# Gate rows of a hybrid decoder block stored in DRAM as 2-KB runs, in four copies side by side

## The chip, the cores and the metric

The kernel runs on one core of one Trainium2 chip. Time is the device time of one execution in microseconds (us). The engines are TensorE (PE; its weight loads are listed apart as PEld), VectorE (DVE), ScalarE (ACT), GpSimd (POOL) and SyncE (SP); SP and POOL issue the DMA transfers, which all run on the core's 16 DMA engines.

## The reference

One layer of a decoder block on 512 tokens with 1024 channels, all in float32. A combined projection of the normalised input gives the operands of two branches. Branch A is a gated delta rule over 8 heads, in chunks of 64 tokens; branch B is causal attention over 8 heads ("FOX") with a forget bias. Both need per-token, per-head gate values, and the change is about how these are spread:

```
u = RMSNorm(x)
[q_A,k_A,v_A,z_A,a_A,b_A | q_B,k_B,v_B,f_B | gate_A,gate_B] = u @ W_in
beta = sigmoid(b_A);  g = -exp(a_log) * softplus(a_A + dt_bias)      # per token and head
A: S_t = a_t (I - beta_t k_t k_t^T) S_{t-1} + beta_t k_t v_t^T,  o_t = S_t^T q_t,  a_t = exp(g_t)
B: softmax(q k^T / sqrt(d) + c_t - c_s),  c = cumsum(log sigmoid(f_B)),  causal
m = sigmoid(gate_A) * (y_A @ P_A) + sigmoid(gate_B) * (y_B @ P_B);  h = x + m @ W_out
out = h + relu(RMSNorm(h) @ W_up)^2 @ W_down
```

The decay between two tokens of a chunk is the exponential of a difference of cumulated g. As a 128x128 block with keys on the partitions and queries along the row, it needs one of the two as a column (a value per partition) and the other as a row that is the same on all partitions.

## The kernel before

Matrix products run on PE with each float32 operand split into a high and a low part (`hi`, `lo`: ACT casts `hi`, DVE subtracts for `lo`) and three products. Weights come as "units" of 128x1024 through three raw buffers. The program is one sequence of units. First come the gates' columns (`w_ab`) and five `z` units, then the projections q, k, v of heads 0 to 3 of branch A (`w_gdn`, lines 281 to 285), the other three `z` units, and a stream of three Strassen chunks with seven products each that makes q, k, v of FOX heads 0 to 3 (`w_sf`, line 986), with the first projections of heads 4 and up in between. A second such stream (`w_st`) makes FOX heads 4 to 7 and the output gates; the block's output projections and the MLP (`mlp`, line 1147) follow. In a chunk some weight quarters are loaded from SP, the others are formed by loads on POOL's queue that add to a raw buffer (`sraw<-w_sf`, line 225).

Beside the units run small tasks (generators) that give way to each other at each unit: `gates`, `decays` for each group of four heads, `head` for each head of branch A, the inversion and scan of a group, and `fox_worker`. The order of the instructions on each engine is then set by a scheduler at build time. Each engine works its instructions in that order.

`gates` turns the gate columns into four kinds of row per head, with 512 tokens each: exp of the cumulated decay (kind 0), beta (1), the centred cumulated decay (2) and minus the cumulated log forget gate (3). It holds them with tokens on the partitions, one column for each kind, chunk of 128 tokens and head. One transpose on PE gives kinds 0 to 2 as 96 rows of 128 tokens (`rowsT`, lines 523 to 525), another kind 3 as 32 rows (`rowsF`). They are stored to DRAM (`rowd`, laid out kind, chunk, head, token), the first from POOL's queue (line 526), the second from SP's (line 546). `row_page` loads one row onto all 128 partitions, from SP (line 550): each partition reads the same four pieces of 512 bytes, which stand 4 KB apart in `rowd`. There are 32 such loads, one for each kind and head.

Their users are: `decays`, where POOL masks kind 2 (`em`, line 585), ACT takes exp (line 589) and POOL multiplies by kind 1 (`eb`, line 591); `head`, where DVE forms `AT` from `eb` (line 644) and POOL multiplies q by kind 0 (`er`, line 655); and `fox_worker`, where POOL masks kind 3 (`nd`, line 884) and ACT adds it as bias. The row pages share four buffers. `head` also has its norm's power on POOL (`ssk`, line 351), between these. Finished operands of a head are stored to DRAM (`hd<-conv`, `hd<-kn`, `hd<-vb`, `hd<-am`, line 148) and come back for the scan; `zc` loads and `oad` stores belong to the scan's output.

Of the kernel before, what the change touches and what calls it, by code (L numbers as in the profile page):

```python
# [7 lines left out]
F32 = mybir.dt.float32  # L8
F32R = mybir.dt.float32r
AF = mybir.ActivationFunctionType  # L10
ALU = mybir.AluOpType
# [4 lines left out]
P = 128  # L16
T = 512
D = 1024
KT = D // P
H = 8  # L20
NCH = T // P
# [5 lines left out]
LA_RAW_MLP = 5  # L27
PER_UNIT = 2
PIN = (400, 400, 0)
NMM = 3  # L30
NZX = 5
DECAY_AT = (9, 1)
# [11 lines left out]
def hybrid_block(tc, a, out):  # L44
    nc = tc.nc
# [6 lines left out]
    drp = ctx.enter_context(tc.tile_pool(name="drp", bufs=1, space=DRAM))  # L52
    mix = ExitStack()
    cm = mix.enter_context(tc.tile_pool(name="cm", bufs=1))
    rwp = mix.enter_context(tc.tile_pool(name="rwp", bufs=4))
# [3 lines left out]
    swp = mix.enter_context(tc.tile_pool(name="swp", bufs=2))  # L59
    pmm = ctx.enter_context(tc.tile_pool(name="pmm", bufs=NMM, space=PSUM))  # L60
    psx = ExitStack()
    pat = psx.enter_context(tc.tile_pool(name="pat", bufs=8 - NMM, space=PSUM))

    n_names = [0]

    def nm(s):
        n_names[0] += 1
        return f"{s}_{n_names[0]}"
# [5 lines left out]
    def page(dt=F32, s="pg"):  # L74
        if s in FOX_TAGS:
            return fxp.tile([P, T], dt, tag=s, name=nm(s))
        tag = TAGS_OF.get(s, s)
        if tag in TAGS:
            return pgp.tile([P, T], dt, tag=tag, name=nm(s), bufs=TAGS[tag])
        return pgp.tile([P, T], dt, tag="pg", name=nm(s))  # L80
# [3 lines left out]
    def const(shape, s, dt=F32):  # L84
        return (cp if s in KEEP else cm).tile(shape, dt, tag=s, name=s)
# [3 lines left out]

    mmfree = [f"mm{i}" for i in range(NMM)]  # L90

# [9 lines left out]
    def atps(s="at"):  # L101
        return pat.tile([P, T], F32, tag="at", name=nm(s))

    def v3(ap, n):
        return ap.rearrange("p (a b) -> p a b", a=n)

    def bc(ap, n):
        return ap.unsqueeze(2).to_broadcast(list(ap.shape) + [n])

    def cs(c):  # L110
        return slice(c * P, (c + 1) * P)

    mm = nc.tensor.matmul
    vec, act, pool = nc.vector, nc.scalar, nc.gpsimd
# [23 lines left out]
    def start(gen):  # L138
        tasks.append(gen)
        return gen  # L140
# [166 lines left out]
    ident = const([P, P], "ident")  # L307
# [52 lines left out]
    def inv_rms(pss, rs, rb):  # L360


        for c in range(NCH):
            vec.tensor_scalar(rs[:, c:c + 1], pss[:, c * 64:c * 64 + 1], 1.0 / D, EPS, op0=ALU.mult, op1=ALU.add)
        rsq(rs, rs)
        yield
        prb = atps("rb")
        for c in range(NCH):
            mm(prb[:, cs(c)], rs[:, c:c + 1].to_broadcast([P, P]), ident, start=True, stop=True)
        act.copy(rb, prb)  # L370
# [21 lines left out]
    for pool_, tag, n in early:  # L392
        t = pool_.tile([P, n * T], F32R, tag=tag, name=nm("xs"))
# [63 lines left out]
    beta = const([P, NCH, H], "beta")  # L457
    gf = const([P, NCH, 16], "gf")
    ngc = const([P, NCH, H], "ngc")
    kds = const([P, NCH, H], "kds")  # L460
    dec = const([P, NCH, H], "dec")
    nbe = const([P, NCH, H], "nbe")
    cc = const([P, NCH, H], "cc")
    rowd = drp.tile([4, NCH, H, P], F32, tag="rowd", name="rowd")

    def rowc(t):
        return t[:, :].unsqueeze(1).to_broadcast([P, NCH, H])

    def gates(ps):
        abT = page(s="abT")  # L470
        act.copy(abT[:64, :], ps[:64, :])
        yield from inv_rms(pss, rs, rb)
        start(normalise())
        yield
        pt = atps("abt")
        for c in range(NCH):
            mm(pt[:, c * 32:(c + 1) * 32], abT[:64, cs(c)], blk_id[0:64, :], start=True, stop=True)
        ab = const([P, NCH, 32], "ab")
        vec.tensor_tensor(ab, v3(pt[:, 0:NCH * 32], NCH), bc(rs[:, :], 32), op=ALU.mult)
        act.activation(beta, ab[:, :, 8:16], AF.Exp, scale=-1.0)  # L480
        aexp = const([P, H], "aexp")
        act.activation(aexp, alog, AF.Exp)
        yy = const([P, NCH, 16], "yy")
        vec.tensor_tensor(yy[:, :, 0:8], ab[:, :, 0:8], rowc(dtb), op=ALU.add)
        vec.tensor_tensor(yy[:, :, 8:16], ab[:, :, 16:24], rowc(fbias), op=ALU.add)
        vec.tensor_scalar(yy[:, :, 8:16], yy[:, :, 8:16], -1.0, None, op0=ALU.mult)

        ee = const([P, NCH, 16], "ee")
        vec.scalar_tensor_tensor(ee, yy, -1.0, yy, op0=ALU.mult, op1=ALU.min)
        act.activation(ee, ee, AF.Exp)  # L490
        yield
        vec.tensor_scalar(beta, beta, 1.0, None, op0=ALU.add)
        vec.reciprocal(beta, beta)
        zz = const([P, NCH, 16], "zz")
        vec.tensor_scalar(zz, ee, 2.0, None, op0=ALU.add)
        vec.reciprocal(zz, zz)
        vec.tensor_tensor(zz, zz, ee, op=ALU.mult)
        vec.tensor_tensor(ee, zz, zz, op=ALU.mult)
        pp = const([P, NCH, 16], "pp")
        vec.tensor_scalar(pp, ee, 1.0 / 19, None, op0=ALU.mult)  # L500
        for k in (17, 15, 13, 11, 9, 7, 5, 3):
            vec.scalar_tensor_tensor(pp, pp, 1.0 / k, ee, op0=ALU.add, op1=ALU.mult)
        vec.scalar_tensor_tensor(pp, pp, 1.0, zz, op0=ALU.add, op1=ALU.mult)
        vec.tensor_scalar(yy, yy, 0.0, None, op0=ALU.max)
        vec.scalar_tensor_tensor(gf, pp, 2.0, yy, op0=ALU.mult, op1=ALU.add)
        vec.scalar_tensor_tensor(gf[:, :, 0:8], gf[:, :, 0:8], -1.0, rowc(aexp), op0=ALU.mult, op1=ALU.mult)
        vec.tensor_scalar(gf[:, :, 8:16], gf[:, :, 8:16], -1.0, None, op0=ALU.mult)
        yield
        pc = atps("cum")
        mm(pc[:, 0:64], upper, gf[:, :, :].rearrange("p a b -> p (a b)"), start=True, stop=True)  # L510
        mm(pc[:, 64:128], ones, gf[:, :, :].rearrange("p a b -> p (a b)"), start=True, stop=True)
        cum = const([P, NCH, 16], "cum")
        vec.tensor_copy(cum, v3(pc[:, 0:64], NCH))
        mm(pc[:, 128:160], mid, gf[:, :, 0:8], start=True, stop=True)
        tot = const([P, NCH, 16], "tot")
        vec.tensor_copy(tot, v3(pc[:, 64:128], NCH))

        rows = const([P, 4, NCH, H], "rows")
        vec.tensor_copy(rows[:, 2], v3(pc[:, 128:160], NCH))
        act.activation(rows[:, 0], cum[:, :, 0:8], AF.Exp)  # L520
        vec.tensor_copy(rows[:, 1], beta)
        pt = atps("rowsT")
        nc.tensor.transpose(pt[:96, 0:P], rows[:, 0:3, :, :].rearrange("p k c h -> p (k c h)"), ident)
        rowsT = const([96, P], "rowsT")
        vec.tensor_copy(rowsT, pt[:96, 0:P])
        nc.gpsimd.dma_start(rowd[0:3, :, :, :].rearrange("k c h t -> (k c h) t"), rowsT)
        vec.tensor_scalar(ngc, rows[:, 2], -1.0, None, op0=ALU.mult)
        yield
        early_rows[0] = True
        vec.tensor_copy(cc[:, 0], cum[:, 0, 8:16])  # L530
        pre = const([P, NCH, H], "pre")
        vec.tensor_copy(pre[:, 1], tot[:, 0, 8:16])
        for c in range(2, NCH):
            vec.tensor_tensor(pre[:, c], pre[:, c - 1], tot[:, c - 1, 8:16], op=ALU.add)
        vec.tensor_tensor(cc[:, 1:], cum[:, 1:, 8:16], pre[:, 1:], op=ALU.add)
        vec.tensor_scalar(rows[:, 3], cc, -1.0, None, op0=ALU.mult)
        vec.tensor_tensor(kds, tot[:, :, 0:8], cum[:, :, 0:8], op=ALU.subtract)
        act.activation(kds, kds, AF.Exp)
        act.activation(dec, tot[:, :, 0:8], AF.Exp)
        vec.scalar_tensor_tensor(nbe, beta, -1.0, rows[:, 0], op0=ALU.mult, op1=ALU.mult)  # L540
        yield
        pt = atps("rowsT")
        nc.tensor.transpose(pt[:32, 0:P], rows[:, 3, :, :].rearrange("p c h -> p (c h)"), ident)
        rowsF = const([32, P], "rowsF")
        vec.tensor_copy(rowsF, pt[:32, 0:P])
        nc.sync.dma_start(rowd[3, :, :, :].rearrange("c h t -> (c h) t"), rowsF)

    def row_tile(src, v=None):
        t = rwp.tile([P, T], F32, tag="row", name=nm("row"))
        nc.sync.dma_start(v3(t[:, :], NCH) if v else t, src)  # L550
        return t

    def row_page(kind, h):
        return row_tile(rowd[kind, :, h, :].partition_broadcast(P), True)


    G = 4
# [655 lines left out]

    pq = ctx.enter_context(tc.tile_pool(name="pq", bufs=8 - NMM, space=PSUM))
    free = [(pq, f"pq{i}") for i in range(8 - NMM)] + [(pmm, tag) for tag in mmfree]

# [149 lines left out]
    for k, (w, c, p, s_) in enumerate(MLP):  # L1366
        for pin, first in zip(pins, PIN):
            pin[0] = k >= first
# [4 lines left out]
        n = pos[0]  # L1373
# [119 lines left out]
```

## Time and profile before

| what | value |
|---|---|
| time, median of 3 runs (lowest to highest) | 982.0 us (980.56 to 983.99) |
| profiled execution: its time, its span | 986.59 us, 984.8 us |
| mean granted PE clock | 0.993 |
| row loads from `rowd` | 32, from 69.9 to 360.7 us |
| DMA, mean over the span | 180 GB/s |

The profile lists, for each engine, when an instruction ran, how long it took, and in brackets how long the engine stood idle before it and what ended that. A group row ends with total busy time and the mean ns of one. A window row has the busy times of PE, PEld, DVE, ACT and POOL with their instruction counts (or of one engine where it is said), then the granted PE clock, the share of the 16 DMA engines' time in use, and GB/s. A DMA's row on SPq or POOLq is its issue, not its transfer; the time to landing is from the issue until the data is there.

### The profile page before, as it was taken

To read this page: it belongs to the slowest core of one execution; us is meant where nothing else is said; L and a number is where in the kernel's file an instruction comes from. 1 tells how busy PE (TensorE), PEld (TensorE's weight loads), DVE (VectorE), ACT (ScalarE), POOL (GpSimd) and SP (SyncE) were. 2 spreads that over 40 slices of the span, in tenths; PEclk is the share of its full clock that TensorE was granted. 3 is DMA by queue.
4 is the path that set the end of the run, shared out by engine and by line. 5 is a ranking of instruction groups with operands and counts; after the bars stand their busy time and mean duration, and the time that the engine had idled before them with its cause. 6 is when DMAs were issued, how large, how long until landed. Compare 5 with 4: busy or idle time off the path is not lost.

```text
span 984.8 us, 17110 instructions
## 1 busy us (share of the span) xinstructions
PE 966.0 (98%) x6460; PEld 868.2 (88%) x6460; DVE 724.8 (74%) x1220; ACT 625.3 (63%) x1086; POOL 231.7 (24%) x232
## 2 busy tenths in 40 slices
PE   8999997999998999999999999999999999999998
PEld 6788787998897899999999888889989989988986
DVE  6877976875557889965656625889897697698596
ACT  6888754687656676777656422578855765666761
POOL 1504221240242423521230004412021121121110
PEclk9999998999999999999999999999999999999999
DMA  7346957763677787777878735678798788889884
GB/s 264 126 138 171 262 144 174 163 183 105 201 225 186 167 202 172 149 167 193 223 174 223 264 107 164 124 184 165 200 182 194 189 170 208 181 173 203 182 165 123
DMA packets 96625, 177.01 MB, mean 180 GB/s; under 512 B 8048, under 2 KB 53264, under 8 KB 96544
## 3 DMA queue, kind: packets, MB, share of 16 engines
q1 hardware_dynamic: 80352, 117.15, 37.9%
q0 software_dynamic: 16192, 58.78, 34.1%
q8 instruction: 51, 0.84, 0.3%
q14 instruction: 30, 0.25, 0.1%
HBM read 156.96 MB, written 18.94 MB: 179 GB/s over the span
## 4 chain that ended last, share of the span: by engine, by line
PE 86%; DMA 4%; DVE 4%; ACT 2%; issue 2%; POOL 1%; SPq 0%; DVEq 0%; POOLq 0%; ACTq 0%
PE mlp L1147 35%; PE st L986 19%; PE mm L281 6%; PE mm L285 6%; PE mm L282 6%; DMA row<-rowd 2%; PE fo L950 2%; PE sc L925 2%; DMA sraw<-w_sf 1%; PE pT L941 1%; PE v L801 1%; DVE conv L602 1%; DMA zc<-zd 1%; PE o L822 1%; DVE lo L263 1%
## 5 line engine op out<-in xcount | busy, mean ns | idle before, releaser
L1378 ACT CAST hi<-draw 128x1024 fp32r<-128x1024 f32 x124 | 130.0, 1050 | 118.5 <-PE mlp L1147 99.5
L1385 DVE TENSOR_TENSOR lo<-draw,hi 128x1024 fp32r<-128x1024 f32 x124 | 151.3, 1223 | 45.7 <-ACT hi L1378 42.5
L262 ACT CAST hi<-sraw 128x1024 fp32r<-128x1024 f32 x70 | 73.2, 1047 | 69.0 <-PE st L986 34.0
L1147 PE MATMUL mlp<-hi,shi 128*128 128x512 f32 x280 | 109.5, 391 | 0.1
L1147 PE MATMUL mlp<-hi,slo 128*128 128x512 f32 x280 | 109.1, 390 | 0.0
L1147 PE MATMUL mlp<-lo,shi 128*128 128x512 f32 x280 | 109.1, 390 | 0.0
L263 DVE TENSOR_TENSOR lo<-sraw,hi 128x1024 fp32r<-128x1024 f32 x70 | 86.9, 1243 | 27.3 <-ACT hi L262 19.6
L1147 PE MATMUL mlp<-slo,hi 128*128 128x256 f32 x448 | 90.3, 283 | 0.0
L1147 PE MATMUL mlp<-shi,lo 128*128 128x256 f32 x448 | 90.3, 283 | 0.0
L1147 PE MATMUL mlp<-shi,hi 128*128 128x256 f32 x448 | 90.3, 283 | 0.0
L281 PE MATMUL mm<-uhi,hi 128*128 128x512 f32 x216 | 85.5, 399 | 2.3 <-ACT hi L262 1.9
L282 PE MATMUL mm<-ulo,hi 128*128 128x512 f32 x216 | 85.7, 399 | 1.3 <-DVE ulo L296 1.3
L262 ACT CAST hi<-raw 128x1024 fp32r<-128x1024 f32 (+1 forms) x50 | 50.3, 1012 | 57.2 <-PE mm L282 46.4
L263 DVE TENSOR_TENSOR lo<-raw,hi 128x1024 fp32r<-128x1024 f32 (+1 forms) x50 | 61.8, 1240 | 26.0 <-ACT hi L262 18.4
L1147 PEld LDWEIGHTS mlp<-shi,hi 128*128 128x128 f32 x448 | 70.6, 192 | 0.9
L1147 PEld LDWEIGHTS mlp<-shi,lo 128*128 128x128 f32 x448 | 69.9, 192 | 0.0
L1147 PEld LDWEIGHTS mlp<-slo,hi 128*128 128x128 f32 x448 | 69.8, 192 | 0.0
L1147 PEld LDWEIGHTS mlp<-lo,shi 128*128 128x128 f32 x280 | 52.6, 188 | 11.3 <-DVE lo L1385 0.2
L1147 PEld LDWEIGHTS mlp<-hi,shi 128*128 128x128 f32 x280 | 52.6, 188 | 11.1 <-issue 0.7
L1147 PEld LDWEIGHTS mlp<-hi,slo 128*128 128x128 f32 x280 | 52.6, 188 | 10.4
L602 DVE SCALAR_TENSOR_TENSOR conv<-mm,c_conv,conv 128x511 f32<-128x511 f32 (+2 forms) x72 | 52.6, 742 | 6.0 <-ACT conv L599 5.6
L225 POOL DMA_DIRECT2D draw<-w_d x30 | 26.3, 878 | 130.4 <-DVE lo L1385 119.8
(331 smaller groups left out, 2386.3 us busy)
## 6 DMA issues: line engine op xcount, KB each, us to landing
draw<-w_u POOLq DMA_DIRECT2D x32, 512.0 KB, 5.7
draw<-w_d POOLq DMA_DIRECT2D x32, 512.0 KB, 6.3
sraw<-w_st POOLq DMA_DIRECT2D x28, 512.0 KB, 6.7
draw<-w_d SPq DMA_DIRECT2D x26, 512.0 KB, 4.4
raw<-w_gdn SPq DMA_DIRECT2D x24, 512.0 KB, 3.9
draw<-w_u SPq DMA_DIRECT2D x24, 512.0 KB, 4.5
sraw<-w_st SPq DMA_DIRECT2D x21, 512.0 KB, 5.0
hd<-hd SPq DMA_DIRECT2D x34, 256.0 KB, 4.8
```

What stands on the lines that cost most here:

```text
L225: nc.gpsimd.dma_start(raw, a[w][c, q, s_], accum_op=ALU.add)
L262: act.copy(hi[:, c], raw[:, c])
L263: vec.tensor_tensor(lo[:, c], raw[:, c], hi[:, c].bitcast(F32), op=ALU.subtract)
L281: mm(o, w, rhi(k), start=(k == 0), stop=False)
L282: mm(o, w, rlo(k), start=False, stop=False)
L285: mm(o, lo[:, k * cols:(k + 1) * cols], rhi(k), start=False, stop=(k == KT - 1))
L602: vec.scalar_tensor_tensor(y[:, s:], ps[:, :T - s], cw[:, i:i + 1], y[:, s:], op0=ALU.mult, op1=ALU.add)
L925: mm(psc[:, :n], qT[:, s], kT[:, :n], start=True, stop=True)
L986: mm(o, u, w, start=first and t == 0 and k == 0 and j == 0 and x is hi, stop=x is lo and k == 3, skip_group_check=True)
L1147: return (lambda *args, **kw: tc.keep_in_program_order(f(*args, **kw))) if self.pinned[0] else f
L1378: pact.copy(hi, raws[m][0])
L1385: pvec.tensor_tensor(lo, raws[m][0], hi[:, :].bitcast(F32), op=ALU.subtract)
```

## The change

The rows get another form in DRAM. The gate columns are held with the chunk outermost and kind and head inside, so that for each chunk one transpose on PE gives 24 rows (kinds 0 to 2) or 8 rows (kind 3) of 128 tokens. Four of these fill one PSUM page of 24 (8) rows by 512 tokens, which DVE copies out. The store then writes each row of 2 KB four times, one copy behind the other (NROW = 4). `row_page` reads for each group of four partitions these four copies, so that a partition reads one run of 2 KB, and partition p reads copy p mod 4. The small intermediates of the gates (`ab`, `yy`, `ee`, `zz`, `pp`, `cum`, `tot`) move from buffers of their own into one page of the common pool, `gates`.

```diff
+NROW = 4
-    rowd = drp.tile([4, NCH, H, P], F32, tag="rowd", name="rowd")
+    rows = const([P, NCH, 4 * H], "rows")
+    rowf = const([40, T], "rowf")
+    rowd = drp.tile([4 * H, NROW, T], F32, tag="rowd", name="rowd")
+
+    def rows_out(eng, kinds, p0):
+        n, k0 = len(kinds) * H, kinds[0] * H
+        pt = atps("rowsT")
+        for c in range(NCH):
+            nc.tensor.transpose(pt[:n, cs(c)], rows[:, c, k0:k0 + n], ident)
+        vec.tensor_copy(rowf[p0:p0 + n, :], pt[:n, :])
+        eng.dma_start(rowd[k0:k0 + n, :, :], rowf[p0:p0 + n, :].unsqueeze(1).to_broadcast([n, NROW, T]))
...
-        pt = atps("rowsT")
-        nc.tensor.transpose(pt[:96, 0:P], rows[:, 0:3, :, :].rearrange("p k c h -> p (k c h)"), ident)
-        rowsT = const([96, P], "rowsT")
-        vec.tensor_copy(rowsT, pt[:96, 0:P])
-        nc.gpsimd.dma_start(rowd[0:3, :, :, :].rearrange("k c h t -> (k c h) t"), rowsT)
+        rows_out(nc.gpsimd, (0, 1, 2), 0)
...
-        pt = atps("rowsT")
-        nc.tensor.transpose(pt[:32, 0:P], rows[:, 3, :, :].rearrange("p c h -> p (c h)"), ident)
-        rowsF = const([32, P], "rowsF")
-        vec.tensor_copy(rowsF, pt[:32, 0:P])
-        nc.sync.dma_start(rowd[3, :, :, :].rearrange("c h t -> (c h) t"), rowsF)
+        rows_out(nc.sync, (3,), 32)
...
     def row_page(kind, h):
-        return row_tile(rowd[kind, :, h, :].partition_broadcast(P), True)
+        t = rwp.tile([P, T], F32, tag="row", name=nm("row"))
+        nc.sync.dma_start(t, rowd[kind * H + h].unsqueeze(0).to_broadcast([P // NROW, NROW, T]))
+        return t
```

Each engine keeps its number of rows in the order (merged rows counted once), and apart from names and shapes the order moves in two places. The first is on DVE, where the first row copy out of PSUM stands among the convolution of the first heads. Before:

```order
L263 TENSOR_TENSOR lo_766<-raw_703,hi_765 128x1024
L525 COPY rowsT<-rowsT_466 96x128
L602 SCALAR_TENSOR_TENSOR conv_656<-mm_631,c_conv,conv_656 128x509
L534 TENSOR_TENSOR pre<-pre,tot 128x8
L602 SCALAR_TENSOR_TENSOR conv_693<-mm_668,c_conv,conv_693 128x511
```

Of the change, on DVE:

```order
L264 TENSOR_TENSOR lo_765<-raw_702,hi_764 128x1024
L602 SCALAR_TENSOR_TENSOR conv_655<-mm_630,c_conv,conv_655 128x509
L536 TENSOR_TENSOR pre<-pre,gates_383 128x8
L474 COPY rowf<-rowsT_461 24x512
L602 SCALAR_TENSOR_TENSOR conv_692<-mm_667,c_conv,conv_692 128x511
```

The copy stands two instructions later. The second place is SP's queue behind the first row loads. Before:

```order
L148 DMA hd_583<-conv_619 128x4x128
L233 DMA raw_1128<-w_z 128x1024
L148 DMA hd_583<-conv_803 128x4x128
L550 DMA row_954<-rowd 128x4x128
L148 DMA hd_583<-am_884 128x4x128
```

Of the change, on SP:

```order
L149 DMA hd_582<-conv_618 128x4x128
L234 DMA raw_1127<-w_z 128x1024
L553 DMA row_953<-rowd 128x1x512
L149 DMA hd_582<-conv_802 128x4x128
L149 DMA hd_582<-am_883 128x4x128
```

One row load goes ahead of a store of a head's operand; the other 31 keep their places in SP's order, as do the transposes on PE, which are four in a row in each of the two places.

More of the change, by code (lines that the diff above doesn't have):

```diff
@@ L477, in gates @@
             mm(pt[:, c * 32:(c + 1) * 32], abT[:64, cs(c)], blk_id[0:64, :], start=True, stop=True)
-        ab = const([P, NCH, 32], "ab")
+        tmp = page(s="gates")
+        ab = v3(tmp[:, 0:P], NCH)
+        yy, ee, zz, pp, cum, tot = [v3(tmp[:, P + 64 * i:P + 64 * i + 64], NCH) for i in range(6)]
         vec.tensor_tensor(ab, v3(pt[:, 0:NCH * 32], NCH), bc(rs[:, :], 32), op=ALU.mult)
@@ L482, in gates @@
         act.activation(aexp, alog, AF.Exp)
-        yy = const([P, NCH, 16], "yy")
         vec.tensor_tensor(yy[:, :, 0:8], ab[:, :, 0:8], rowc(dtb), op=ALU.add)
@@ L486, in gates @@
         vec.tensor_scalar(yy[:, :, 8:16], yy[:, :, 8:16], -1.0, None, op0=ALU.mult)
-        ee = const([P, NCH, 16], "ee")
         vec.scalar_tensor_tensor(ee, yy, -1.0, yy, op0=ALU.mult, op1=ALU.min)
@@ L493, in gates @@
         vec.reciprocal(beta, beta)
-        zz = const([P, NCH, 16], "zz")
         vec.tensor_scalar(zz, ee, 2.0, None, op0=ALU.add)
@@ L498, in gates @@
         vec.tensor_tensor(ee, zz, zz, op=ALU.mult)
-        pp = const([P, NCH, 16], "pp")
         vec.tensor_scalar(pp, ee, 1.0 / 19, None, op0=ALU.mult)
@@ L511, in gates @@
         mm(pc[:, 64:128], ones, gf[:, :, :].rearrange("p a b -> p (a b)"), start=True, stop=True)
-        cum = const([P, NCH, 16], "cum")
         vec.tensor_copy(cum, v3(pc[:, 0:64], NCH))
         mm(pc[:, 128:160], mid, gf[:, :, 0:8], start=True, stop=True)
-        tot = const([P, NCH, 16], "tot")
         vec.tensor_copy(tot, v3(pc[:, 64:128], NCH))
[L518 to L521, printed above, removed]
-        pt = atps("rowsT")
-        nc.tensor.transpose(pt[:96, 0:P], rows[:, 0:3, :, :].rearrange("p k c h -> p (k c h)"), ident)
-        rowsT = const([96, P], "rowsT")
-        vec.tensor_copy(rowsT, pt[:96, 0:P])
-        nc.gpsimd.dma_start(rowd[0:3, :, :, :].rearrange("k c h t -> (k c h) t"), rowsT)
-        vec.tensor_scalar(ngc, rows[:, 2], -1.0, None, op0=ALU.mult)
+        vec.tensor_copy(rows[:, :, 2 * H:3 * H], v3(pc[:, 128:160], NCH))
+        act.activation(rows[:, :, 0:H], cum[:, :, 0:8], AF.Exp)
+        vec.tensor_copy(rows[:, :, H:2 * H], beta)
+        rows_out(nc.gpsimd, (0, 1, 2), 0)
+        vec.tensor_scalar(ngc, rows[:, :, 2 * H:3 * H], -1.0, None, op0=ALU.mult)
         yield
@@ L535, in gates @@
         vec.tensor_tensor(cc[:, 1:], cum[:, 1:, 8:16], pre[:, 1:], op=ALU.add)
-        vec.tensor_scalar(rows[:, 3], cc, -1.0, None, op0=ALU.mult)
+        vec.tensor_scalar(rows[:, :, 3 * H:], cc, -1.0, None, op0=ALU.mult)
         vec.tensor_tensor(kds, tot[:, :, 0:8], cum[:, :, 0:8], op=ALU.subtract)
@@ L539, in gates @@
         act.activation(dec, tot[:, :, 0:8], AF.Exp)
-        vec.scalar_tensor_tensor(nbe, beta, -1.0, rows[:, 0], op0=ALU.mult, op1=ALU.mult)
+        vec.scalar_tensor_tensor(nbe, beta, -1.0, rows[:, :, 0:H], op0=ALU.mult, op1=ALU.mult)
         yield
-        pt = atps("rowsT")
-        nc.tensor.transpose(pt[:32, 0:P], rows[:, 3, :, :].rearrange("p c h -> p (c h)"), ident)
-        rowsF = const([32, P], "rowsF")
-        vec.tensor_copy(rowsF, pt[:32, 0:P])
-        nc.sync.dma_start(rowd[3, :, :, :].rearrange("c h t -> (c h) t"), rowsF)
+        rows_out(nc.sync, (3,), 32)
     def row_tile(src, v=None):
```

## The prediction

> **What bounds the kernel now.** I read the page's busy times first, then TensorE's own waits in the timeline, the chain of waits behind each, and the DMA rows.
>
> ```profile
> span 984.8 us, 17110 instructions
> PE 966.0 (98%) x6460; PEld 868.2 (88%) x6460; DVE 724.8 (74%) x1220; ACT 625.3 (63%) x1086; POOL 231.7 (24%) x232
> ```
>
> TensorE (PE) is the bound: it stands still for 984.8 - 966.0 = 18.8 us in all. A change to gate rows can only win what stands still between 70 us (first row load) and 361 us (last), or what such a stop costs afterwards. In that stretch the PE timeline has three stops of note:
>
> ```profile
> 116.86 0.47 PE L281 MATMUL mm<-uhi,hi 128*128 128x512 f32 x1 [1.88 <-ACT hi L262]
> 167.30 1.23 PE L986 MATMUL st<-hi,uhi 128*128 128x256 f32 x4 [5.43 <-ACT fqk L966]
> 302.93 1.12 PE L119 MATMUL ktm<-ident,conv 128*128 128x128 f32 x4 [2.31 <-ACT conv L604]
> ```
>
> I call them A (1.88), B (5.43) and C (2.31): 9.6 us. After B and C the granted clock (PEclk, the third number from the right) also falls; a table of 2-us windows, PE alone, shows it:
>
> ```profile
> 168.00:170.00 2.00, 2.00 (x11) 0.50 0.61 238
> 170.00:172.00 2.00, 2.00 (x12) 0.50 0.61 51
> 172.00:174.00 2.00, 2.00 (x15) 0.74 0.94 174
> 304.00:306.00 2.00, 2.00 (x7) 0.50 0.70 171
> ```
>
> Half the clock for 2 us loses 1.0 us. B so costs 1.0 + 1.0 + 0.5 = 2.5 us more, C at least 1.0. The whole that the change can reach is 9.6 + 3.5 = 13.1 us.
>
> Now the row loads. The list of DMA issues (size of each, median us from issue to landing):
>
> ```profile
> row<-rowd SPq DMA_DIRECT2D x32, 256.0 KB, 7.0
> hd<-hd SPq DMA_DIRECT2D x34, 256.0 KB, 4.8
> zc<-zd SPq DMA_DIRECT2D x8, 256.0 KB, 5.9
> ```
>
> All move 256 KB. A table of chosen windows shows why the rows are slowest; the last two numbers are the DMA share and GB/s:
>
> ```profile
> 146.00:150.00 4.00, 4.00 (x33) 3.90 (x32) 3.73 (x5) 3.77 (x7) 1.06 (x2) 1.00 1.10 289
> 150.50:154.50 4.00, 4.00 (x35) 4.00 (x35) 3.90 (x9) 2.00 (x3) 2.01 (x3) 1.00 0.82 89
> 155.00:160.00 5.00, 5.00 (x44) 5.00 (x43) 2.98 (x9) 0.00 (x0) 0.00 (x0) 1.00 1.07 233
> 128.50:132.50 4.00, 4.00 (x18) 3.02 (x17) 4.00 (x8) 3.26 (x5) 0.95 (x1) 1.00 0.28 46
> 71.50:76.00 4.50, 4.50 (x29) 3.84 (x28) 0.62 (x3) 2.85 (x16) 0.41 (x1) 1.00 0.32 58
> 257.50:258.50 1.00, 1.00 (x10) 0.96 (x9) 0.00 (x0) 0.59 (x2) 0.92 (x2) 1.00 0.83 262
> 264.00:264.80 0.80, 0.80 (x9) 0.80 (x9) 0.49 (x2) 0.00 (x0) 0.00 (x0) 1.00 0.94 333
> ```
>
> Rows 2, 4 and 5 are the stretches in which row loads were the oldest work in the queue: 46 to 89 GB/s, with other transfers waiting behind. The sixth holds mostly zc loads, which also come in 512-byte pieces, but each partition from its own place: 262 GB/s. The last holds hd loads in 2-KB pieces: 333 GB/s. So 512-byte pieces as such are not slow; pieces that all 128 partitions read from the same 2 KB are. At 58 GB/s a page of 256 KB holds the queue 4.5 us, at 262 it would be 1.0, at 333 0.8.
>
> **The change part by part.** *Loads.* 32 loads of 512 pieces become 32 of 128 pieces of 2 KB, read out of 8 KB instead of 2. The trace holds no broadcast read of that form. Bounds: 0.8 us of queue per page (the hd row) below, and no better than now, 4.5 us, above; worse is possible too, and its nearest rows are the slowest loads of before, one in the first burst of four and one alone at 94.3 us (least, median and longest from issue to landing, of all row loads and of that one):
>
> ```profile
> DMA to landing us min/median/max: 3.3/7.0/14.9
> DMA to landing us min/median/max: 9.3/9.3/9.3
> ```
>
> I take 1.5 us, a saving of 3 us for a page that stands alone in the way, because same size and direction put it nearest to the zc and hd rows once four places share the readers.
>
> The Trainium skill (DMA: Bandwidth & Descriptors, section Specifications) sets 512 B as the smallest transfer at line rate. By that rule the loads of before are at line rate already, the saving is next to nothing and the sum below is about +0.6 us. The zc and hd windows agree with it, the three row windows do not.
>
> *Stop A.* The chain of waits, start and length:
>
> ```profile
> 71.07 12.46 DMA row<-rowd
> 83.55 7.10 DMA row<-rowd
> 90.81 1.27 POOL conv L655
> 92.08 2.23 POOL eb L591
> 94.42 1.02 POOL ssk L351
> ```
>
> The third of the first four rows lands at 83.5, and SP's queue issues the next row (er, for q times er) right behind that landing; the issues ahead of it had been slow themselves, 2.4 to 2.7 us each (start and length):
>
> ```profile
> 75.46 2.70 SPq L546 DMA_DIRECT2D rowd<-rowsF  x1
> 78.27 2.41 SPq L233 DMA_DIRECT2D raw<-w_gdn  x1
> 80.77 2.69 SPq L148 DMA_DIRECT2D hd<-kn  x1
> 83.55 0.83 SPq L550 DMA_DIRECT2D row<-rowd  x1
> ```
>
> The burst of four took some 15 us. With pages of 1.5 us it takes 6, so that er, which then waits for its free buffer and for kn on DVE, lands at about 85 instead of 90.65, and POOL reaches ssk some 1.5 us sooner, as soon as ScalarE has the squares for it. DVE and ScalarE then gain up to the 1.88 us that PE stood still. I book -1.5 (bounds +1.2, if nothing is faster and the start is later, and -1.9).
>
> *Stop B.* What PE waited for was a weight load with accumulation:
>
> ```profile
> 147.69 1.09 SPq L550 DMA_DIRECT2D row<-rowd  x1
> 151.41 12.77 DMA sraw<-w_sf
> ```
>
> The row was issued ahead of it, and 150.5 to 154.5 is the 89 GB/s window above; then the accumulating loads run at 233. A page 3 us shorter lets sraw land up to 3 us sooner; I book -2.5, since some accumulating packets did move meanwhile. That leaves a stop of 2.9, longer than C, after which the clock fell, so I book nothing for the clock (bounds 0 and -7.9, all of B).
>
> The skill (TensorE: Matmul & The Clock Gate, Part 1) lets the clock fall after an idle window of about 3.4 us. By that rule a stop of 2.9 keeps the clock, and B would give another -2.5. C, 2.31 us long with the clock at 0.50 behind it, speaks against counting on it.
>
> *Stop C.* ScalarE stood 5.58 us for the landing of a store whose page it needed:
>
> ```profile
> 286.29 0.36 SPq L550 DMA_DIRECT2D row<-rowd  x1
> 286.70 0.56 SPq L148 DMA_DIRECT2D hd<-kn  x1
> 294.14 0.69 ACT L599 ACTIVATE conv<-mm,c_conv 128x512 f32<-128x512 f32 x1 [5.58 <-DMA hd<-kn]
> ```
>
> The store was issued right behind a row. Landing 3 us sooner covers the 2.31 us stop and its 1.0 us of clock; other work on ScalarE and POOL lies between, so I book -2.5 of 3.3 (bounds 0 and -3.3).
>
> *What it adds.* Two transposes become eight, each set of four like this one, which took 0.44 us to the next row:
>
> ```profile
> 74.39 0.60 PE L119 MATMUL vtm<-ident,conv 128*128 128x128 f32 x4
> 65.37 0.28 DVE L525 COPY rowsT<-rowsT 96x128 f32<-96x128 f32 x1
> L813 DVE COPY st<-S 128x512 f32<-128x512 f32 x2 | 1.4, 683 | 0.0
> L602 DVE SCALAR_TENSOR_TENSOR conv<-mm,c_conv,conv 128x511 f32<-128x511 f32 (+2 forms) x72 | 52.6, 742 | 6.0 <-ACT conv L599 5.6
> rowd<-rowsT POOLq DMA_DIRECT2D x1, 48.0 KB, 3.3
> ```
>
> Six more at 0.11 are +0.6 on PE, which is the bound: booked in full. Each copy out of PSUM goes from 0.28 to about 0.68 (the 512-wide copy), and the first one starts behind one conv row (0.74) and a small sum, some 0.7 later; with a store of 192 KB instead of 48 the first rows can be fetched about 1.2 to 1.5 us later. PE has projections queued until A, so this is 0 by itself; if the pages are no faster, A pays it (the +1.2). The other gate instructions keep count, size and place. The one load that now goes ahead of a conv store on SP moves by one issue, 0.4 us: nothing.
>
> Sum: -1.5 - 2.5 - 2.5 + 0.6 = -5.9 us. The profiled run took 986.6 in all (1.8 around the span), 4.6 above the median of the three timed runs, 982.0; I apply the difference to the median: 976.
>
> **The rivals.** A measurement of this kernel can tell about 0.3% from no change, 2.9 us: faster is below 979.1, slower above 984.9.
>
> *R1, the pages stay slow.* If all engines walk through the copies in the same order, they read one copy at a time, and the place is as crowded as now; 4.5 us a page stays. For it: no row here shows a broadcast of 2-KB runs. Against it: 58 GB/s comes with 512-byte reads scattered over four places 4 KB apart, and runs four times as long ask four times less often. Time: 982 + 0.6, about 982.5. The skill's descriptor swizzle (same DMA page, The descriptor swizzle) has each engine write four neighbouring partitions in turn, which would be just this order; no run here shows it.
>
> *R2, the pages are faster but B stays.* Three accumulating loads of 512 KB stand in line at B, and 155 to 160 shows them at 233 GB/s with a DMA share of 1.07: if they are limited by their own adding, sraw lands when it did. A and C give -4.0, less 0.6: about 979.
>
> *R3, slower.* The four copies lie in 8 KB side by side, the four pieces of before 4 KB apart. If nearness crowds the memory more, a page goes from a landing of 7.0 to, say, 9.3 (the load at 94.3), +2.3 at each of A, B and C, and the start's +1.2 at A: about +8 with the transposes, 990. It decides from a median landing above about 8 us. Against it: the hd row, whose 2-KB runs move best of all.
>
> **How the numbers follow.** Forecast (pages faster, all three stops shrink) 0.49, at 976, own range 970 to 979.5; R2 0.17 at 979; R1 0.20 at 982.5; R3 0.14 at 990. Faster: nearly all of the forecast, half of R2 and a tenth of R1, 0.59. Same: the rest of R2, most of R1, 0.26. Slower: R3 and a little of R1, 0.15. The range, 969 to 985, takes in the forecast with most of its lower bound (13.1 us off, 0.6 on, is 969.5), R2 and R1, and leaves out R3.
>
> **What would show it.** Right: row<-rowd lands in a median of 3.5 to 5 us; no window of 4 us in which row loads run under 100 GB/s; POOL's q times er at head 0 starts near 85 instead of 90.8; B's sraw lands in 9 to 10 us and B is near 3; ScalarE's wait for hd<-kn near 287 is under 3 us and C is gone. Wrong: row landings still near 7 (R1) or above 8 (R3); or landings near 4 and B still above 5 (R2). My sum would also be wrong if a stop of PE appeared where now there is none.

## The result, and the profile after

| kernel | time, median of its runs (lowest to highest) | profiled execution, span | mean granted PE clock |
|---|---|---|---|
| before, run beside the changed kernel | 982.09 us (980.56 to 983.99) | 986.59 us, 984.8 us | 0.993 |
| changed | 972.84 us (972.55 to 974.02) | 972.55 us, 970.8 us | 0.999 |

The changed kernel is faster: the ratio of its time to that of the kernel before is 0.9907, with a 95% interval of 0.9888 to 0.9926. That is 9.2 us, where I had forecast 6.

The page of the changed kernel, its first lines:

```profile
span 970.8 us, 17121 instructions
PE 960.3 (99%) x6466; PEld 864.7 (89%) x6466; DVE 723.4 (75%) x1220; ACT 625.0 (64%) x1086; POOL 230.6 (24%) x232
```

PE now stands still for 970.8 - 960.3 = 10.5 us, where it stood 18.8. Its timeline between 40 and 310 us, every row with an idle time of 0.2 us or more in front of it (in brackets, with what ended it):

```profile
46.30 0.50 PE L283 MATMUL mm<-ulo,hi 128*128 128x512 f32 x1 [1.32 <-DVE ulo L297]
186.08 0.33 PE L941 MATMUL pT<-ident,p 128*128 128x128 f32 x1 [0.40 <-DVE p L938]
201.55 0.44 PE L904 MATMUL fqT<-ident,fqk 128*128 128x128 f32 x2 [0.24 <-POOL fqk L895]
303.11 0.47 PE L282 MATMUL mm<-uhi,hi 128*128 128x512 f32 x1 [1.21 <-DVE conv L602]
```

A, B and C are gone. What stands at 303.11 is not C made smaller: C waited for ScalarE in front of a transpose, and this row waits for a convolution on DVE, one step further. The same row in the trace of the kernel before, with the row that answers to 46.30:

```profile
47.89 0.50 PE L282 MATMUL mm<-ulo,hi 128*128 128x512 f32 x1 [1.32 <-DVE ulo L296]
316.90 0.47 PE L281 MATMUL mm<-uhi,hi 128*128 128x512 f32 x1 [0.25 <-DVE conv L602]
```

So this stop grew from 0.25 to 1.21 us (what that stands against is told under C, below). And 47.89 - 46.30 = 1.59 us of the difference between the two profiles arose before the first row was loaded; the change has no part in it: in the profile of before the clock was at about half from 9.2 to 12.6 us, which loses 1.7 us, and in that of the changed kernel it was not. Behind B and C the clock no longer falls either. The same three windows after B, PE alone, in the changed kernel:

```profile
168.00:170.00 2.00, 2.00 (x19) 1.00 0.99 180
170.00:172.00 2.00, 2.00 (x19) 1.00 0.95 178
172.00:174.00 2.00, 2.00 (x19) 1.00 1.02 190
```

The DMA issues of the changed kernel, with the median time to landing in us at the end:

```profile
row<-rowd SPq DMA_DIRECT2D x32, 256.0 KB, 3.7
hd<-kn SPq DMA_DIRECT2D x8, 256.0 KB, 3.6
zc<-zd SPq DMA_DIRECT2D x8, 256.0 KB, 5.3
rowd<-rowf POOLq DMA_DIRECT2D x1, 192.0 KB, 3.3
```

The rows land in 3.7 us instead of 7.0, and so does what stands beside them: the stores `hd<-kn` took 6.3 us before and take 3.6, though the change does not touch them. Their row before:

```profile
hd<-kn SPq DMA_DIRECT2D x8, 256.0 KB, 6.3
```

The `zc` loads went only from 5.9 to 5.3. In the three stretches that the prediction quoted as slow, the last number (GB/s) is now:

```profile
71.50:76.00 4.50, 4.50 (x30) 3.82 (x29) 1.36 (x3) 3.81 (x19) 1.33 (x2) 1.00 0.95 291
128.50:132.50 4.00, 4.00 (x22) 3.36 (x21) 3.88 (x9) 1.55 (x2) 0.00 (x0) 1.00 1.05 279
150.50:154.50 4.00, 4.00 (x36) 4.00 (x35) 3.79 (x9) 0.74 (x3) 1.10 (x2) 1.00 1.07 208
```

They had 58, 46 and 89 GB/s. These are the same times and no longer the same work: in the second and third no row load is under way any more. The loads themselves tell it better. The first four rows landed after 7.0 to 14.9 us and land after 3.2 to 4.7; the row in front of the second stretch (issued at 125.68, now at 122.68) went from 8.1 to 3.3, and the row ahead of B (147.69, now 143.70) from 8.2 to 3.4. The single waits that the prediction had named look like this now (POOL's q times `er` of head 0, and ScalarE's wait for the landing of `kn`, each from its engine's timeline, and the least, median and longest landing time of the loads of `sraw` issued from 140 to 165 us):

```profile
82.80 1.29 POOL L655 TENSOR_TENSOR conv<-conv,row 128x512 f32<-128x512 f32 x1 [1.63 <-PE kq L650]
280.12 0.69 ACT L599 ACTIVATE conv<-mm,c_conv 128x512 f32<-128x512 f32 x1 [2.04 <-DMA hd<-kn]
DMA to landing us min/median/max: 4.4/5.7/6.9
```

q times `er` starts at 82.8 instead of 90.8 and waits for a matrix product, no longer for a row; ScalarE's wait fell from 5.58 to 2.04 us. Five of the eight loads in the last line are accumulating ones; they take 5.7 to 6.9 us, where the four issued in the same stretch of before took 6.1 to 13.3.

### The profile page after: what moved, and what is told of

Its sections match the earlier page's. It is cut to its first block, busy times and chain, and to the rows that moved or that the text cites. A ratio compares the mean times of both kernels' runs of the same rounds, so it can differ in the third digit from the quotient of the medians.

```text
span 970.8 us, 17121 instructions
## 1 busy us (share of the span) xinstructions
PE 960.3 (99%) x6466; PEld 864.7 (89%) x6466; DVE 723.4 (75%) x1220; ACT 625.0 (64%) x1086; POOL 230.6 (24%) x232
## 4 chain that ended last, share of the span: by engine, by line
PE 91%; DVE 4%; ACT 2%; issue 2%; POOL 1%; DMA 1%; SPq 0%; DVEq 0%; POOLq 0%; ACTq 0%
PE mlp L1147 36%; PE st L986 19%; PE mm L282 8%; PE mm L286 8%; PE mm L283 8%; PE fo L950 2%; PE sc L925 2%; PE pT L941 1%; PE o L822 1%; PE v L801 1%; DVE lo L264 1%; PE w L793 1%; PE S L810 1%; PE kq L650 1%; PE kk L642 1%
## 5 line engine op out<-in xcount | busy, mean ns | idle before, releaser
L286 PE MATMUL mm<-uhi,lo 128*128 128x512 f32 x216 | 56.9, 398 | 0.0
```

The source lines that it names most:

```text
L286: mm(o, lo[:, k * cols:(k + 1) * cols], rhi(k), start=False, stop=(k == KT - 1))
```

## The experiments

What the result leaves open is why the old rows were slow. Three things changed at once: the length of a piece (512 bytes to 2 KB), the number of places that the readers share (one to four), and the distance of a row's pieces (4 KB to none). The prediction blamed the second. Two other questions are which rows mattered, and whether the rest of the change (wider transposes, the page for the intermediates) did anything. In all kernels but one (told below) the code is the changed kernel's, and the order of the instructions is kept but for a few places on SP's queue.

### One copy, and pieces of 512 bytes

One copy of the 2-KB run, all partitions reading the same place:

```diff
-NROW = 4
+NROW = 1
```

> 2-KB runs kept, but one copy of each row instead of four: all 128 partitions read the same 2 KB, in 128 pieces instead of 512. Place theory (the row loads were slow because all partitions read the same 2 KB): pages stay slow, median landing 6 us or more, windows with row loads alone in front under 110 GB/s, stops of TensorE come back, time 979 to 984 us. Piece theory (they were slow because of 512 pieces each): landing 3.5 to 4.2 us, no stop of TensorE between 60 and 360 us, time 972 to 974 us.

Measured: 974.88 us (974.73 to 975.3), ratio to the kernel before 0.9909 (0.9886 to 0.9933); median landing of a row 4.9 us. The prediction's cause, that all partitions read one place, is not what cost 9 us. One place costs 1.2 us in the landing. In the time it is 2 us by the medians, but the kernel before had 983.75 us beside this run and 982.09 beside the changed kernel, and by the two ratios (0.9909 and 0.9907) it is almost nothing. The other half of the same question, four copies in pieces of 512 bytes, 1 KB apart:

```diff
-    rowd = drp.tile([4 * H, NROW, T], F32, tag="rowd", name="rowd")
+    rowd = drp.tile([4 * H, NROW * NCH, 2 * P], F32, tag="rowd", name="rowd")
...
-        nc.sync.dma_start(t, rowd[kind * H + h].unsqueeze(0).to_broadcast([P // NROW, NROW, T]))
+        nc.sync.dma_start(v3(t[:, :], NCH), rowd[kind * H + h, :, 0:P].unsqueeze(0)
+                          .to_broadcast([P // NROW, NROW * NCH, P]))
```

> Four copies of each row kept, but each copy lies in DRAM as four pieces of 512 bytes with 512 bytes of gap between them, so that a load again has 512 pieces, out of 16 places 1 KB apart. The stores become four DMAs of a quarter each. Place theory: pages move at 200 GB/s or more, landing 3.5 to 5 us, time 972 to 976 us. Piece theory: landing near 7 us as before the change, time 980 to 983 us.

Measured: 974.58 us (972.46 to 975.82), ratio 0.9905 (0.9881 to 0.9928), median landing 4.3 us. Small pieces are not the cause either. Each theory by itself had failed, and what neither run had kept was the distance of 4 KB.

### Which kinds of row matter

Kind 3 in the old layout, kinds 0 to 2 as changed:

```diff
+    rowd3 = drp.tile([NCH, H, P], F32, tag="rowd3", name="rowd3")
...
+        if kinds == (3,):
+            eng.dma_start(rowd3.rearrange("c h t -> h c t"), v3(rowf[p0:p0 + n, :], NCH))
+            return
...
+        if kind == 3:
+            return row_tile(rowd3[:, h, :].partition_broadcast(P), True)
```

> The eight rows of kind 3 (forget bias of branch B) go back to the DRAM form of before, one copy in pieces of 512 bytes 4 KB apart; kinds 0 to 2 keep four copies. My attribution: stop B (sraw behind the kind-3 row issued near 148 us) comes back with 2 to 5 us and its clock loss, A and C stay away; time 975 to 979 us. Rival (all three stops hang on the crowded stretch of the first heads, and B vanished because everything ran earlier): B stays away, time 972 to 974 us.

Measured: 974.85 us (972.45 to 975.05), ratio 0.9904 (0.9881 to 0.9927). B did not come back, and neither did A or C; the time lies just under the 975 to 979 us that I had expected. But the run does not say what I had meant it to say: SP's row issue just ahead of the accumulating loads, and the two lines that issue rows in this kernel (L553 for kind 3, L560 for the others), stand in its trace as follows:

```profile
L560 SPq DMA_DIRECT2D row<-rowd x24: 512/519/640, 68.8 to 289.2; - x24
L553 SPq DMA_DIRECT2D row<-rowd x8: 359/538/912, 103.2 to 348.7; - x8
143.61 0.55 SPq L560 DMA_DIRECT2D row<-rowd  x1
```

The row at B comes from the line for kinds 0 to 2, so it was a fast row in this run. That B hangs on a row of kind 3 is refuted; that it hangs on the row issued ahead of it is not. The other way round, kinds 0 to 2 in the old layout and kind 3 as changed:

```diff
+    rowd0 = drp.tile([3, NCH, H, P], F32, tag="rowd0", name="rowd0")
...
+        if 3 not in kinds:
+            for k in kinds:
+                eng.dma_start(rowd0[k].rearrange("c h t -> h c t"), v3(rowf[k * H:k * H + H, :], NCH))
+            return
...
+        if kind < 3:
+            return row_tile(rowd0[kind, :, h, :].partition_broadcast(P), True)
```

> The 24 rows of kinds 0 to 2 (branch A) go back to the DRAM form of before; kind 3 keeps four copies. The store becomes three DMAs on POOL's queue. My attribution: A and C come back (1 to 2 and 2 to 3 us, with C's clock loss), B stays away or shrinks under 3 us; time 976 to 980 us. Rival: only B hung on the rows, A and C were the noise of one execution; time 972 to 974 us.

Measured: 981.61 us (980.34 to 983.54), ratio 0.998 (0.9967 to 0.9992). Nearly all of the gain is gone (more than the 976 to 980 us of my attribution), so it belongs to kinds 0 to 2. Its PE timeline, the stops over 1 us from 110 to 315 us:

```profile
116.56 0.47 PE L282 MATMUL mm<-uhi,hi 128*128 128x512 f32 x1 [1.97 <-ACT hi L263]
164.08 0.74 PE L994 MATMUL st<-hi,uhi 128*128 128x256 f32 x4 [1.14 <-ACT fqk L974]
299.72 0.66 PE L120 MATMUL ktm<-ident,conv 128*128 128x128 f32 x4 [2.30 <-ACT conv L612]
313.67 0.47 PE L282 MATMUL mm<-uhi,hi 128*128 128x512 f32 x1 [1.41 <-DVE conv L610]
```

A, B and C are all back, by name and waiter; B is 1.14 us here, with a second stop of 0.76 us ten microseconds later. In this run the clock fell behind A, not behind B or C.

### The distance of the pieces

Five runs read a row as pieces of 512 bytes and differ in their distance and in the number of copies (with it in the number of stores) alone. The first is the run with four copies above; the others change one number of it:

```diff
-NROW = 4
+NROW = 1
...
-    rowd = drp.tile([4 * H, NROW * NCH, 2 * P], F32, tag="rowd", name="rowd")
+    rowd = drp.tile([4 * H, NROW * NCH, 8 * P], F32, tag="rowd", name="rowd")
```

The first half alone is one copy 1 KB apart, the second alone four copies 4 KB apart, both together one copy 4 KB apart, and `9 * P` in place of `8 * P` one copy 4.5 KB apart.

> One copy of each row, and that copy as four 512-byte pieces 1 KB apart: as in the run with four copies of such pieces (974.58 us, median landing 4.3 us), but all 128 partitions read the same four pieces, as they did in the old form, whose pieces stood 4 KB apart. Two theories of what made the old rows slow are left after the runs with one copy in one 2-KB run and with four copies in 512-byte pieces, which were both fast. Pitch theory: it is the 4 KB between the pieces of a row. Then this run is fast: 973.5 to 976.5 us, median landing of a row 4 to 5.2 us, no stop of PE over 1.5 us between 110 and 310 us. Both-together theory: it takes small pieces and one place for all partitions, either alone is harmless. Then this run is slow: 979.5 to 983 us, median landing 6 us or more, and the stops near 117 us and 300 us are back with about 2 us each.

> Four copies of each row, each as four 512-byte pieces, but all sixteen pieces stand 4 KB apart (64 KB for a row) where the run that took 974.58 us had 1 KB between them. Each piece is read by 32 partitions, as there. Pitch theory: the 4 KB between the pieces makes rows slow: 979.5 to 983 us, median landing of a row 6 us or more, the stops of PE near 117 and 300 us back. Both-together theory (small pieces and one place for all partitions): this run is fast, 973.5 to 976.5 us, median landing 4 to 5.2 us.

> One copy of each row as four 512-byte pieces 4 KB apart, which is the old form's reading of a row, with all else as in the changed kernel; only the heads do not stand between each other's pieces as they did before. Pitch theory and both-together theory expect the same: slow, 980 to 983.5 us, median landing 6 us or more. If it is fast (below 977 us), neither holds as stated, and what made the old rows slow is something else in their layout: that the pieces of eight heads and three kinds stood interleaved in 48 KB, or the many 512-byte writes that put them there.

> One copy of each row as four 512-byte pieces 4.5 KB apart, where the run with 4 KB took 979.09 us and the one with 1 KB 974.08 us. Theory that a distance of just 4 KB lets a row's pieces and its neighbours fall on the same part of the memory: 4.5 KB is fast, 973.5 to 976 us, median landing 4 to 5.2 us. Theory that pieces far apart are slow at any distance: 978 to 981 us, median landing 6 us or more.

| copies | distance of the 512-byte pieces | time, us (lowest to highest) | ratio to before (95%) | landing of a row, median us |
|---|---|---|---|---|
| 4 | 1 KB | 974.58 (972.46 to 975.82) | 0.9905 (0.9881 to 0.9928) | 4.3 |
| 1 | 1 KB | 974.08 (973.0 to 974.72) | 0.9907 (0.9892 to 0.9922) | 5.0 |
| 1 | 4.5 KB | 974.71 (973.32 to 974.94) | 0.9917 (0.9902 to 0.9933) | 4.5 |
| 4 | 4 KB | 979.07 (978.65 to 979.52) | 0.9959 (0.9944 to 0.9974) | 6.9 |
| 1 | 4 KB | 979.09 (978.5 to 982.2) | 0.9957 (0.9941 to 0.9974) | 7.4 |

The distance decides, and the copies do nothing for it: at 4 KB four copies are as slow as one, at 1 KB one is as fast as four. Nor is it that far pieces are slow: 4.5 KB is as good as 1 KB. Of the three distances only 4 KB is slow; 2 KB, 8 KB and other multiples were not tried. The rows of the issue list that carry this, of four copies 4 KB apart and then of one copy 4.5 KB apart:

```profile
row<-rowd SPq DMA_DIRECT2D x32, 256.0 KB, 6.9
hd<-kn SPq DMA_DIRECT2D x8, 256.0 KB, 5.8
```

```profile
row<-rowd SPq DMA_DIRECT2D x32, 256.0 KB, 4.5
hd<-kn SPq DMA_DIRECT2D x8, 256.0 KB, 4.0
```

The Trainium skill (DMA: Bandwidth & Descriptors, section Latency and other measured facts) tells that copies within DRAM fall from 207 GB/s with the partitions' rows 512 KiB apart to 103 with 4 MiB, and that 4 KiB of padding brings the full rate back; it takes the cause, memory channels that coincide, for an inference. These runs show a loss of that kind at 4 KB, for reads that many partitions share, and that 512 bytes of padding are enough there. They do not show the cause inside the memory.

Both runs at 4 KB came out just under the 979.5 to 983 and 980 to 983.5 us expected of them, and one of the stops expected back is not there. C is (2.32 us with four copies, 2.22 with one), and so is a smaller B (1.19 and 1.47 us, each with another stop of 0.84 and 1.54 us ten microseconds later), but A is not. One copy 4 KB apart took 979.1 us, the old layout 981.6 us for three kinds (above). In the old layout the pieces of eight heads stand between each other as well; what that adds (the two differ by 2.5 us) was not tried by itself. The traces show what the old layout has beyond the two runs at 4 KB: A, 1.97 us there, and one fall of the clock behind it, 1.7 us.

### The rest of the change, and the cheapest edit

The changed kernel with all rows in the old layout, so that only the transposes, the copies out of PSUM and the page for the intermediates remain of the change:

```diff
-    rowd = drp.tile([4 * H, NROW, T], F32, tag="rowd", name="rowd")
+    rowd = drp.tile([4, NCH, H, P], F32, tag="rowd", name="rowd")
...
-        eng.dma_start(rowd[k0:k0 + n, :, :], rowf[p0:p0 + n, :].unsqueeze(1).to_broadcast([n, NROW, T]))
+        for i, k in enumerate(kinds):
+            eng.dma_start(rowd[k].rearrange("c h t -> h c t"), v3(rowf[p0 + i * H:p0 + i * H + H, :], NCH))
```

> The changed kernel with all four kinds of rows in the old layout in DRAM (pieces of 512 bytes, 4 KB apart, the heads' pieces between each other's); the wider transposes, the shared scratch page for the gates and everything else of the change stay. Layout theory: the whole gain is the layout in DRAM, and the kernel before loses nothing by its other forms: 981.5 to 984.5 us, ratio to the kernel before 0.998 to 1.002, median landing of a row 6.4 to 7.2 us, stops of PE of about 2 us near 117 and 300 us and one of over 2 us near 165 us. Rival, that half of the 9 us comes from the rest of the change (one copy with pieces 4 KB apart took 979.1 us, where the kernel before took 983.7 us): 978 to 980.5 us.

Measured: 981.57 us (980.41 to 983.34), ratio 0.9994 (0.9981 to 1.0008). Within that interval the whole gain is the layout. This run is also the cleanest picture of the stops, since its profile starts like the changed kernel's (its row that answers to 46.30 stands at 46.18). Its PE timeline:

```profile
115.61 0.47 PE L282 MATMUL mm<-uhi,hi 128*128 128x512 f32 x1 [1.68 <-ACT hi L263]
162.88 0.74 PE L985 MATMUL st<-hi,uhi 128*128 128x256 f32 x4 [2.30 <-ACT fqk L965]
298.64 0.66 PE L120 MATMUL ktm<-ident,conv 128*128 128x128 f32 x4 [2.18 <-ACT conv L603]
312.60 0.47 PE L282 MATMUL mm<-uhi,hi 128*128 128x512 f32 x1 [1.42 <-DVE conv L601]
```

and its 2-us windows behind B, PE alone, with the granted clock third from the right:

```profile
164.00:166.00 2.00, 2.00 (x13) 0.58 0.39 156
166.00:168.00 2.00, 2.00 (x12) 0.56 0.71 100
```

A, B and C are 1.68 + 2.30 + 2.18 = 6.2 us, and the clock behind B loses 0.84 + 0.88 = 1.7 us: 7.9 of the 9.9 us between this span (980.7) and the changed kernel's (970.8). Two stops that the changed kernel has too are longer here, 1.42 us at 312.60 (1.21 there) and 0.97 us at 192.65 in front of a transpose in the attention of branch B (0.40 there), which makes 8.7. B's accumulating load, in the chain of waits, took 9.65 us:

```profile
81.52 8.90 DMA row<-rowd
150.12 9.65 DMA sraw<-w_sf
```

Last the other way, the kernel before with the one edit that puts a row's four pieces behind one another (one copy, as few transposes as before):

```diff
-    rowd = drp.tile([4, NCH, H, P], F32, tag="rowd", name="rowd")
+    rowd = drp.tile([4, H, NCH, P], F32, tag="rowd", name="rowd")
...
-        rows = const([P, 4, NCH, H], "rows")
+        rowk = const([P, 4, H, NCH], "rows")
+        rows = rowk.rearrange("p k h c -> p k c h")
...
-        return row_tile(rowd[kind, :, h, :].partition_broadcast(P), True)
+        return row_tile(rowd[kind, h, :, :].partition_broadcast(P), True)
```

(The two transposes and stores take `rowk` in its own order.)

> The kernel before, with one thing changed: in DRAM a row's four pieces of 512 bytes stand one behind the other (2 KB in one run, one copy) where they stood 4 KB apart; the transposes are as few as before, and no copy is added. Layout theory: this alone takes the gain of the run with one copy in a 2-KB run in the changed kernel: 972.5 to 975.5 us, median landing of a row 4.5 to 5.2 us. Rival, that half of the gain comes from the rest of the change (the scratch of the gates, the wider transposes): 977 to 980 us.

Measured: 974.0 us (972.51 to 975.63), ratio 0.9914 (0.9896 to 0.9931), median landing 4.5 us. Beside it on the same chip the changed kernel again:

> The changed kernel unaltered, beside the others on one chip, to tell whether its four copies are worth anything over one copy. If copies count (place theory in part): 972 to 973.5 us and at least 1 us below the kernel before with its pieces put together. If only the distance of the pieces counts: within 1 us of it. In both cases ratio to the kernel before 0.989 to 0.993.

Measured: 972.57 us (972.42 to 974.77), ratio 0.9902 (0.9886 to 0.9918), median landing of a row 3.7 us. The changed kernel stands 1.4 us lower, but the two sets of runs overlap, so this pair alone does not settle that the copies pay. All four kernels with one copy and a harmless distance had medians from 974.0 to 974.9 us, the changed kernel 972.84 and 972.57 us: I take some 1.5 us for the copies as likely, not as shown. The traces have a place for it: these four kernels have a stop of 0.60 to 1.19 us near 168 us, behind an accumulating load, and one of 0.96 to 0.98 us near 188 us; the changed kernel has no stop at the first place in either trace, and 0.40 and 0.35 us at the second. Four copies alone do not take these stops away: the run with four copies in pieces of 512 bytes 1 KB apart has them, with 1.24 and 0.98 us. No kernel tried beats the changed one.

### Sixteen copies

```diff
-NROW = 4
+NROW = 16
```

> Sixteen copies of each row side by side, each a 2-KB run (32 KB read in order, where the changed kernel reads 8 KB four... 32 partitions to a copy; here 8 partitions to a copy). Place theory: fewer partitions at a place are faster still, median landing of a row 3.3 us or less where four copies had 3.7 us and one copy 4.9 us; what PE still stops for (1.21 us at 303) is not a row, so the time gains at most 0.5 us: 972 to 973.5 us. Saturation theory: with four copies a row is bound by its 256 KB and the queue; the landing stays 3.5 to 4.0 us, and the larger store (768 KB for three kinds where it was 192 KB) lets the first rows come later: 972.5 to 975 us.

Measured: 977.53 us (975.76 to 977.87), ratio 0.994 (0.9924 to 0.9955): slower than with four, and beyond what either theory allowed. The tile's own view gives the issues and the store's landing, and the timelines of POOL and PE what follows:

```profile
L553 SPq DMA_DIRECT2D row<-rowd x32: 577/600/1112, 74.9 to 351.1; - x32
DMA to landing us min/median/max: 8.3/8.3/8.3
91.15 2.27 POOL L655 TENSOR_TENSOR conv<-conv,row 128x512 f32<-128x512 f32 x1 [7.24 <-ACT hi L263]
116.28 0.47 PE L282 MATMUL mm<-uhi,hi 128*128 128x512 f32 x1 [1.11 <-ACT hi L263]
```

The store of 768 KB lands after 8.3 us (3.3 with four copies), the first row is issued at 74.9 instead of 68.8, q times `er` starts at 91.15, and A is back with 1.11 us. This is the mechanism that the prediction held ready as A's +1.2, at a larger store. Against the changed kernel it is 4.7 us by the medians and 3.2 us by the ratios (0.994 and 0.9907). A and the small stops behind it are some 2.2 us more than in the changed kernel, and 1.1 us of the two profiles' 4.6 us is an earlier difference at the start (47.40 against 46.30); the rest I did not trace, and whether sixteen places help the rows themselves stays open, since their landing is not in this trace.

## Why the prediction was right, and where it was not

**Direction and range.** Faster by over 0.3% was the forecast, and it came; 972.84 lies inside the range of 969 to 985 and inside the forecast's own range of 970 to 979.5. The three rivals fell by the marks that had been set for them: landings of 3.7 us (not near 7, R1; not above 8, R3) and no B (R2). Two signs of being right were missed on the good side: `sraw` was to land in 9 to 10 us with B near 3, and its loads there land in 5.7 to 6.9 us with no B. And a stop did grow where the sum had none, the one at 303.11.

**The cause of the slow rows.** "Pieces that all 128 partitions read from the same 2 KB are slow" was wrong. The reading of the windows behind it was sound (58 GB/s against 262 for distinct pieces of 512 bytes), but I drew the line between the two cases at the shared place, and the table of distances shows that it runs at 4 KB. I had that number in hand: the pieces "4 KB apart" are named in R1 and R3, there as something harmless or even helpful. The forecast held because the change undid the distance along with the rest. A change that had only added copies, at 4 KB, would have been forecast near 976 and would have come out near 979.

**A.** Right in its chain, and nearly in size: booked 1.5 of 1.88 us, and all of it went. Over the kernels, A is there when q times `er` starts late (before, 90.79 us: 1.88; three kinds old, 91.57 us: 1.97; all old, 90.56 us: 1.68; sixteen copies, 91.15 us: 1.11). It is not there at 82.80, nor at the 87.99 and 88.83 us of the two runs with 4 KB, whose rows are slow as well.

**B.** The term that was mis-sized. The mechanism, a row ahead of the accumulating loads, stands: in the nine traces in which that row is fast, the slowest accumulating load issued from 140 to 165 us lands after 6.5 to 8.6 us, in the five in which it is slow after 10.2 to 13.3. But I let the page's 3 us be all that the load could gain, kept a stop of 2.9 us and booked nothing for the clock; the stop went altogether, and the clock with it. In the profiled execution of before, B and its clock were worth 5.43 + 2.5 = 7.9 us, in the run with the old layout 2.30 + 1.7 = 4.0, with the three kinds old 1.14 + 0.76. B varies from run to run; the profile that I worked from held a large one, which fits its time lying 4.6 us above the median. Taking the old-layout run for an ordinary execution, which is my estimate, the booked 2.5 was short by about 1.5, not by 5.4.

**C.** Right: the wait for `kn` fell from 5.58 to 2.04 us and the stop and its clock went (booked 2.5 of 3.3). The clock behind C was priced at 1.0 from one window; it stayed at half until 306 us and lost about 1.6. That belongs to this one execution: the four other runs with C (2.18 to 2.32 us) kept a clock of 1.00 behind it. What I had not listed is the next convolution, 0.25 us in the profile of before and 1.21 at 303.11. It does not come of C's going, since those four runs have 1.41 to 1.43 us at that place beside a full C. I read the 0.25 as the other side of the slow clock: PE, working at half speed behind C, came later to that row. That is argued from these traces and was not tried.

**The adds.** Six more transposes were booked at +0.6 us. The run that keeps them and the old layout has a ratio of 0.9994 (0.9981 to 1.0008), which is 0.6 us below the kernel before, with an interval of 1.9 below to 0.8 above. By the total an addition of 0.6 us can be neither shown nor refuted, but PE's timeline shows it. The first set of transposes and the row behind it, before and then in the changed kernel:

```profile
63.72 0.27 PE L523 MATMUL rowsT<-ident,rows 128*96 128x128 f32 x1
63.75 0.48 PE L281 MATMUL mm<-uhi,hi 128*128 128x512 f32 x1
62.16 0.60 PE L473 MATMUL rowsT<-ident,rows 128*24 128x128 f32 x4
62.52 0.48 PE L282 MATMUL mm<-uhi,hi 128*128 128x512 f32 x1
```

The next row starts 0.03 us behind the single transpose and 0.36 us behind the four; at the second set it is 0.10 and 0.44. That is 0.67 us more in all, close to the 0.6 booked. In the old-layout run A follows, a wait of PE for something else, and it may have taken part of the 0.67 in; no run separates that.

**The sum.** Booked -5.9, measured -9.2 (interval 7.3 to 11.0 by the ratio). The forecast was 3.3 us short. The old-layout run has the six transposes too, so the 9.9 us of span between it and the changed kernel stand against the 6.5 booked for A, B and C, which is 3.4 short. Of the 9.9, A is 1.7, B with its clock 4.0, C 2.2, and the two smaller stops (at 192.65 and 312.60) another 0.8. So 1.5 of the shortfall is B with its clock (4.0 where 2.5 was booked), A and C together came out as booked (3.9 for 4.0), 0.8 is the two stops that were not listed, and some 1.2 us stay without a place.

## What to carry to other kernels

When a broadcast load is slow, write down the addresses that one partition reads before blaming their size or their sharing: here four pieces exactly 4 KB apart cost some 5 us of a 980-us kernel through 32 row loads, and 512 bytes of padding, or putting the pieces behind one another, undid that. A slow transfer is paid by the transfers beside and behind it, so price the waits of the neighbours (`kn`, `sraw`), not the load's own user alone. And check how a stop varies before you book it from one execution: a profile 4.6 us above the median has its surplus somewhere, here in the very stop that was to be won and in falls of the clock at the start and behind C.

## What the runs showed of the hardware that I had not expected

- Pieces of 512 bytes read by many partitions are slow at a distance of 4 KB (median landing of a row 6.9 to 7.4 us) and not at 1 KB or 4.5 KB (4.3 to 5.0 us), whether 128 or 32 partitions read each piece (at 4.5 KB only 128 was tried).
- More copies can cost more than they give: the store of 768 KB of copies landed after 8.3 us instead of 3.3, and the kernel took 4.7 us more than with four copies by the medians (977.53 and 972.84 us), 3.2 by the ratios, of which longer stops of PE explain 2.2.
- The granted clock does not follow the length of a stop alone. It fell to about half behind stops of 2.30 us (B, old layout), 2.31 us (C, before) and 1.97 us (A, three kinds old), and stayed at 1.00 behind one of 2.32 us (C, four copies 4 KB apart). In the profile of before it also fell at 9.2 us, where PE had stopped three times since 5.7 us, for 0.27, 0.79 and 0.46 us. Each fall lost about 1.7 us, some 3.4 us at half (B of before: two of them on end). The rows behind the third and the fourth of the first four stops, PE alone:

```profile
118.00:120.00 2.00, 2.00 (x7) 0.50 0.59 182
```

```profile
297.00:299.00 2.00, 2.00 (x10) 1.00 0.50 147
```

The Trainium skill (TensorE: Matmul & The Clock Gate, Part 1) has the clock fall after an idle window of about 3.4 us, and has these windows run freely, without a start of their own for each kernel. The length of the falls agrees with 3.4 us, and that a stop of one length has both outcomes fits windows that run freely. That 1.97 us was enough, and less than that at 9.2 us, does not fit a rule by which a whole window has to be idle.
